# Four column pairs of an input projection as seven-product block multiplications, with two intermediate results kept in DRAM

## The chip, the core and the metric

The kernel runs as one program on 1 core of one Trainium2 chip. The metric is the device time of one execution in microseconds. TensorE (PE) multiplies matrices; its weight loads (PEld) overlap its matmuls. VectorE (DVE) and ScalarE (ACT) do the elementwise work, and SyncE (SP) issues the transfers. Each engine works through its own list of instructions in the order in which the program was compiled, and waits at an instruction until what it needs is there.

## The reference, cut to what matters

One encoder layer is applied to two groups of 256 tokens, which the kernel holds together as 512 tokens of width 1024. The changed part is the middle: one input projection of the normed activations `u`, whose columns feed a neighbourhood attention (q, k, v), a memory attention (q_m) and a state-space branch.

```python
x = x + 0.5 * swiglu(rms_norm(x, ffn1_norm), ffn1_w_gate, ffn1_w_up, ffn1_w_down)
u = rms_norm(x, mix_norm)
proj = u @ w_in
q_na, k_na, v_na, q_mem, z, xbc, dt_raw, gate_logits = split_sizes(proj, IN_SIZES)
...
o_na = neighborhood_attention(q_na, k_na, v_na, na_rpb)
...
o_mem = memory_attention(q_m, k_m, v_m)
g_na, g_ssd, g_mem = split_sizes(jax.nn.sigmoid(gate_logits), (D_MODEL, D_MODEL, D_MODEL))
merged = g_na * (o_na @ w_br_na) + g_ssd * (o_ssd @ w_br_ssd) + g_mem * (o_mem @ w_br_mem)
x = x + merged @ w_out
x = x + 0.5 * swiglu(rms_norm(x, ffn2_norm), ffn2_w_gate, ffn2_w_up, ffn2_w_down)
```

The q, k, v and q_mem columns are 4 x 1024 columns of `w_in`, 1024 rows deep.

## The kernel before

**Weights.** `PLAN` is a list of entries; each entry multiplies one or more weight chunks of 128 x 1024 numbers (`Item`). A chunk is loaded by SP into a ring of 9 buffers (`fetch`, `wr`), up to 8 items ahead. `ahead` splits it into a high part (`wh`, a cast on ACT, L332) and a low part (`wl`, a subtraction on DVE, L236), up to three items ahead of the one that is multiplied: the pool `pw` has 3 buffers of each. Every product is three matmuls: high by high, high by low, low by high.

**The two ways to multiply.** `quad` (L605 to L607) takes 512 columns: 4 chunks, 4 token blocks, 96 matmuls of 512 columns for 512 tokens by 1024 rows by 512 columns. The feed-forward layers use `product` (L583) instead: a pair of column blocks and a pair of token blocks are combined by seven products in place of eight. Sums of weight chunks are made in place on DVE (`sums`, `wr<-wr,wr`, L236), and the accumulating PSUM banks (`ac`) are shared by several products.

**The middle part.** After the memory's keys and values (`km`, `vm`, which read the memory tokens) and the 64 `dt` columns, eight `quad`s follow: qm 0, qm 1, v 0, v 1, q 0, k 0, q 1, k 1. Then come the memory gates and branches (`gate`, `br`), and after them the convolution columns.

**Background tasks.** Attention and norms are generators in a queue (`later`). `step` advances up to three active tasks by one part each. `run` calls it once after every plan entry, and `product` once more in its middle. The tasks here are `t_qkm` (norm and transposes of q_m, `tr`), `t_am` (memory attention of a head and a group: scores `am`, softmax `pm`, transposes `amT`, output `amo`), `t_qkn` (norms of q and k), `t_na` (neighbourhood attention of a pair of heads: transposes `qT` and `kT`, scaled query `qbd`, scores `ns`, softmax `nt`, transposes `nT`, copies `npT`, output `no`) and `t_dt` (the `dt` columns: `row`, `loc`). `require` runs tasks until those named are done.

**Order and buffers.** The Tile framework orders the instructions of each engine when the program is built. PSUM has 8 banks: 5 in pool `pm` (`m`, `q`, `ac`) and 3 in `pd` (all banks of tasks). Before, the outputs of the attention (`om`, `on`) are split where they are made, and stay in SBUF; so does the memory's v (`vm`). Four pairs of `on` borrow buffers of the weights' ring (`LEND`, `lent`).

Of the kernel before, what the change touches and what calls it, by code (L numbers as in the profile page):

```python
# [51 lines left out]
def seven(p, key, block, nh):  # L52
# [6 lines left out]
    for h in range(nh):  # L59
        n = lambda b: f"gu{key}.{h}.{b}"  # L60
# [6 lines left out]
        out.append(("gu", (*key, p, h, nh), [it]))  # L67
# [3 lines left out]
def make_plan():  # L71
# [10 lines left out]
    def ffn(f):  # L82
# [5 lines left out]
        for ci, (c0, w) in enumerate(CBLOCKS + ((DFF, 0),)):  # L88
# [7 lines left out]
            def part(p, ci=ci, c0=c0, w=w, n=n):  # L96
                s.extend(seven(p, (f, ci), lambda i, j, h: (f + ("_w_up", "_w_gate")[j], 4 * i + 4 // n * h, 4 // n, c0, w), n))
# [83 lines left out]
KEEP, EARLY, PG, LEND = 6, 4, 54, 4  # L181
TEMPS = set("rw e f e2 ca cb xt yq dg jk jn pm pmT nt npT bi st qbd kT nv mq ut mr a2h a2l s1 u2 p5 up sg af sf".split())


class Layer:
    def __init__(self, tc, ctx, aps):
# [20 lines left out]
        self.lent = 0  # L207
# [179 lines left out]
    def setup(self):  # L387
# [36 lines left out]
        self.scr_x = self.dr.tile([KD, 128, NT], F32, name="scr_x")  # L424
        self.scr_v = self.dr.tile([NT, D], F32, name="scr_v")
# [48 lines left out]
    def t_x(self, k):  # L474
# [24 lines left out]
        self.xs[7][k // 2] = self.split_tile(s7, "s")  # L499

# [66 lines left out]
    def product(self, p, h, nh, cis, w):  # L567
# [230 lines left out]
    def do_vm(self, key, cis):  # L798
# [4 lines left out]
        def evac():  # L803
            for t in range(4):
# [5 lines left out]
                self.o[("vm", key[0], t)] = r  # L810
# [48 lines left out]
    def t_am(self, h, b):  # L859
        qT, kT = self.o["qm"], self.o["km"]  # L860
# [29 lines left out]
        for ct in range(2):  # L890
            c0 = (h % 2) * 256 + ct * 128
            for kt in range(2):
                self.T.matmul(ps[:, ct * 256:(ct + 1) * 256], self.o[("vm", h // 2, 2 * b + kt)][:, c0:c0 + 128],  # L893
                              pT[:, kt * 256:(kt + 1) * 256], start=kt == 0, stop=kt == 1)
        for ct in range(2):
            k = ("om", 2 * h + ct)
            if k not in self.o:
                self.o[k] = (self.g(F32R, "omh"), self.g(F32R, "oml"))
            hi, lo = self.o[k]
            v = ps[:, ct * 256:(ct + 1) * 256]  # L900
            self.S.copy(hi[:, bs], v)
# [566 lines left out]
```

## Time and profile before

| | |
|---|---|
| median of 3 runs | 1736.32 us (1736.07 to 1737.01) |
| profiled execution, its own time | 1735.51 us |
| its span, first to last instruction | 1733.7 us |
| PE busy | 1724.5 us |
| DVE busy | 1225.5 us |
| ACT busy | 846.8 us |
| the eight quads, start to end | 456.8 to 682.2 us |
| memory gates and branches | 682.2 to 823.1 us |

The span is what the views divide up; the profiled execution's own time is 1.8 us longer, for what lies around the span. Busy matmuls overlap: each is listed with its whole duration, and the next starts before it ends.

### The profile page before, as it was taken

How to read it: one execution, taken by the hardware profiler on the slowest of the kernel's cores; microseconds unless marked ns; L12 is line 12 of the kernel's file. 1: busy time of each engine (PE TensorE's matmuls, PEld its weight loads, DVE VectorE, ACT ScalarE, POOL GpSimd, SP SyncE). 2: the span in 40 equal slices, each digit the busy share in tenths (PEclk: the TensorE clock that was granted, in tenths of full speed). 3: DMA queues.
4: the chain of work that ended last, by engine and by line, in shares of the span. 5: the costliest groups of instructions: out<-in, count | busy, mean ns of one | idle time of the engine just before them, and what ended most of it. 6: DMA issues, size and time to landing. Idle time of an engine off the chain costs nothing.

```text
span 1733.7 us, 22579 instructions
## 1 busy us (share of the span) xinstructions
PE 1724.5 (99%) x8556; PEld 1419.7 (82%) x8556; DVE 1225.5 (71%) x2057; ACT 846.8 (49%) x1515; POOL 0.8 (0%) x6
## 2 busy tenths in 40 slices
PE   9999999999999999999999999999999999999999
PEld 7888888988888887788878877877788878888887
DVE  7776776876255467845788898888853797776775
ACT  6543443543234336543656776767532564444442
POOL 0000000000000000000000000000000000000000
PEclk9999999999999999999999999999999999999999
DMA  7144234442323233333444544447443234244331
GB/s 273 59 136 146 97 110 134 158 156 82 99 87 96 87 109 91 99 104 98 122 127 128 145 131 120 152 128 200 158 134 121 73 124 132 86 146 133 98 109 49
DMA packets 79852, 209.75 MB, mean 121 GB/s; under 512 B 11136, under 2 KB 19840, under 8 KB 79744
## 3 DMA queue, kind: packets, MB, share of 16 engines
q1 hardware_dynamic: 79744, 208.32, 38.5%
q8 instruction: 67, 1.10, 0.3%
q14 instruction: 41, 0.34, 0.1%
HBM read 198.71 MB, written 9.58 MB: 120 GB/s over the span
## 4 chain that ended last, share of the span: by engine, by line
PE 97%; DVE 2%; ACT 0%; issue 0%; DMA 0%; POOL 0%; DVEq 0%; ACTq 0%; POOLq 0%
PE ac L583 21%; PE m L561 10%; PE m L563 10%; PE m L562 10%; PE q L605 5%; PE q L607 5%; PE q L606 5%; PE m L1110 5%; PE d L562 5%; PE d L563 5%; PE d L561 5%; PE y L1330 2%; PE hT L708 1%; PE am L865 1%; PE amo L893 1%; PE CB L1280 1%
## 5 line engine op out<-in xcount | busy, mean ns | idle before, releaser
L332 ACT CAST wh<-wr 128x1024 fp32r<-128x1024 f32 (+1 forms) x356 | 370.5, 1041 | 676.8 <-PE ac L583 166.5
L236 DVE TENSOR_TENSOR wl<-wr,wh 128x1024 fp32r<-128x1024 f32 (+1 forms) x356 | 430.6, 1210 | 256.6 <-ACT wh L332 243.9
L583 PE MATMUL ac<-wh,sh 128*128 128x512 f32 (+1 forms) x616 | 229.4, 373 | 0.5 <-ACT wh L332 0.5
L561 PE MATMUL m<-uh,wh 128*128 128x512 f32 x576 | 229.7, 399 | 0.0
L583 PE MATMUL ac<-wl,sh 128*128 128x512 f32 (+1 forms) x616 | 228.1, 370 | 0.7 <-DVE wl L236 0.7
L583 PE MATMUL ac<-wh,sl 128*128 128x512 f32 (+1 forms) x616 | 227.9, 370 | 0.0
L563 PE MATMUL m<-uh,wl 128*128 128x512 f32 x576 | 225.0, 391 | 0.0
L562 PE MATMUL m<-ul,wh 128*128 128x512 f32 x576 | 224.8, 390 | 0.0
L562 PE MATMUL d<-hl,wh 128*128 128x512 f32 x352 | 137.3, 390 | 0.7 <-DVE hl L236 0.7
L561 PE MATMUL d<-hh,wh 128*128 128x512 f32 x352 | 137.4, 390 | 0.5 <-ACT hh L258 0.5
L563 PE MATMUL d<-hh,wl 128*128 128x512 f32 x352 | 137.0, 389 | 0.0
L583 PEld LDWEIGHTS ac<-wl,sh 128*128 128x128 f32 x616 | 116.1, 189 | 20.7 <-DVE wl L236 1.3
L583 PEld LDWEIGHTS ac<-wh,sh 128*128 128x128 f32 x616 | 116.0, 188 | 20.5 <-ACT wh L332 1.3
L583 PEld LDWEIGHTS ac<-wh,sl 128*128 128x128 f32 x616 | 116.0, 188 | 19.6
L561 PEld LDWEIGHTS m<-uh,wh 128*128 128x128 f32 x576 | 108.2, 188 | 27.8 <-ACT ct L251 5.0
L563 PEld LDWEIGHTS m<-uh,wl 128*128 128x128 f32 x576 | 108.1, 188 | 23.5 <-issue 0.8
L562 PEld LDWEIGHTS m<-ul,wh 128*128 128x128 f32 x576 | 108.3, 188 | 21.8 <-issue 0.4
L247 DVE SCALAR_TENSOR_TENSOR x<-d,x 128x512 f32<-128x512 f32 x96 | 66.1, 689 | 76.6 <-PE d L563 76.1
L605 PE MATMUL q<-wh,uh 128*128 128x512 f32 x256 | 102.9, 402 | 0.0
L236 DVE TENSOR_TENSOR wr<-wr,wr 128x1024 f32<-128x1024 f32 x80 | 97.5, 1220 | 6.5 <-DMA wr<-in_w 5.4
L607 PE MATMUL q<-wl,uh 128*128 128x512 f32 x256 | 99.9, 390 | 0.0
L606 PE MATMUL q<-wh,ul 128*128 128x512 f32 x256 | 99.9, 390 | 0.0
(260 smaller groups left out, 2856.0 us busy)
## 6 DMA issues: line engine op xcount, KB each, us to landing
wr<-in_w SPq DMA_DIRECT2D x308, 512.0 KB
rw<-scr_r SPq DMA_DIRECT2D x64, 256.0 KB
nv<-scr_v SPq DMA_DIRECT2D x64, 64.0 KB
scr_o<-cv SPq DMA_DIRECT2D x12, 256.0 KB
or<-scr_o SPq DMA_DIRECT2D x12, 256.0 KB
wr<-in_w SPq DMA_DIRECT2D x9, 256.0 KB
x<-in_xT SPq DMA_DIRECT2D x8, 256.0 KB
mr<-in_memT SPq DMA_DIRECT2D x8, 256.0 KB
```

The source lines that it names most:

```text
L236: self.V.tensor_tensor(out=out, in0=a, in1=b, op=op)
L247: self.V.scalar_tensor_tensor(out=out, in0=a, scalar=s, in1=b, op0=op0, op1=op1)
L332: self.S.copy(hi[:, :n], t[:, :n])
L561: self.T.matmul(ps[:m], wh[:, kk, :], xh, start=i == 0, stop=False)
L562: self.T.matmul(ps[:m], wh[:, kk, :], xl, start=False, stop=False)
L563: self.T.matmul(ps[:m], wl[:, kk, :], xh, start=False, stop=i == n - 1)
L583: go = lambda l, r, **f: self.T.matmul(ps, l, r, skip_group_check=True, **f)
L605: self.T.matmul(self.qb[t], xh, wh[:, kk, :], start=k == 0, stop=False)
L606: self.T.matmul(self.qb[t], xl, wh[:, kk, :], start=False, stop=False)
L607: self.T.matmul(self.qb[t], xh, wl[:, kk, :], start=False, stop=k == KD - 1)
L1110: go = lambda l, r, **f: self.T.matmul(ps, l, r, skip_group_check=True, **f)
L1330: T.matmul(yb[64 * hp:64 * hp + 64, b * 256:(b + 1) * 256], xt[i][:, (2 * b + st) * 128 + 64 * hp:(2 * b + st) * 128 + 64 * hp + 64], w[hp ...
```

## The change

The eight quads become four sets of seven products, each for a pair of column blocks: (qm 0, qm 1), (v 0, v 1), (q 0, k 0), (q 1, k 1). A set is 14 plan entries (`sv`, seven products in two halves of the depth), and the seventh product of each set is issued after the first of the next; that of the last set stands after the first memory gate. Memory branches start two gates later. The token sums that products 5, 6, 3 and 7 need are made in `t_u` (`s_part`), before the `dt` columns. The memory's v goes to DRAM (`scr_m`), and `t_am` loads what it needs (`vl`). The outputs of both attentions are written to DRAM unsplit (`scr_b`), and `t_back` loads them and splits them later. The lending of ring buffers is gone. One product entry calls `step` twice, as in the feed-forward layers.

```diff
     quad("vm", 1, "w_mem_kv", 1536)
     a("dt", 0, "w_in", COL_DT, m=64)
-    quad("qm", 0, "w_in", COL_QM)
-    quad("qm", 1, "w_in", COL_QM + 512)
-    quad("v", 0, "w_in", COL_V)
-    quad("v", 1, "w_in", COL_V + 512)
-    for hf in range(2):
-        quad("q", hf, "w_in", 512 * hf)
-        quad("k", hf, "w_in", 1024 + 512 * hf)
+    sets = [("qm", 0, COL_QM, COL_QM + 512), ("v", 0, COL_V, COL_V + 512), ("qk", 0, 0, 1024), ("qk", 1, 512, 1536)]
+
+    def sv(i, p):
+        kind, c, *cols = sets[i]
+        s.extend(seven("sv", p, (kind, c), lambda i, j, h: ("w_in", 4 * i + 2 * h, 2, cols[j], 512), 2))
+
+    for i in range(4):
+        for p in PRODUCTS[:-1]:
+            sv(i, p)
+            if p == 1 and i:
+                sv(i - 1, 4)
     for j in range(8):
         gate("mem", j)
-        branch("mem", j)
+        if j == 0:
+            sv(3, 4)
+        if j > 1:
+            branch("mem", j - 2)
+    branch("mem", 6)
+    branch("mem", 7)
     light = [(f, j) for j in range(8) for f in (gate, branch)]
     for g in range(8):
         for i, (ct, col) in enumerate(((16 + g, COL_B + 128 * g), (24 + g, COL_C + 128 * g), (2 * g, COL_X + 256 * g),
...
         self.stt(lo, s2, -1.0, hi.bitcast(F32), ALU.mult, ALU.subtract)
         self.xs[3][k // 2] = (hi, lo)
         self.xs[7][k // 2] = self.split_tile(s7, "s")
+
+    def s_part(self, k, a, b):
+
+        half = lambda z: z[:, k % 2 * 256:k % 2 * 256 + 256]
+        if k % 2 == 0:
+            self.sf = [self.g(p="sf") for _ in range(4)]
+        s5, s2, s7, s3 = self.sf
+        self.tt(half(s5), b[:, 256:], a[:, 256:], ALU.subtract)
+        self.stt(half(s2), half(s5), -1.0, a[:, :256], ALU.mult, ALU.subtract)
+        self.tt(half(s7), a[:, :256], a[:, 256:], ALU.subtract)
+        self.stt(half(s3), half(s2), -1.0, b[:, :256], ALU.mult, ALU.subtract)
+        if k % 2:
+            for p, z in ((5, s5), (6, s2), (3, s3), (7, s7)):
+                self.su.setdefault(p, [None, None])[k // 2] = self.split_tile(z, "s")
+
+    def factor_of(self, p, k, t):
+
+        if self.base is None or p in self.su:
+            pair, c = (self.xs if self.base is None else self.su)[p][k // 2], k % 2 * 256
+        else:
+            k0, r = {1: (0, 0), 2: (4, 0), 4: (4, 1)}[p]
+            pair, c = self.base[k0 + k], 256 * r
+        return (z[:, c + t * 128:c + t * 128 + 128] for z in pair)
 
     def t_squares(self):
         for k in range(KD):
...
         yield from self.t_R(acc)
         yield
-        self.u = []
-        for k in range(KD):
-            t = self.g(p="ut")
-            self.stt(t, self.x[k], self.par("mix", k), self.R, ALU.mult, ALU.mult)
-            self.u.append(self.split_tile(t, "u"))
-            self.nc.sync.dma_start(out=self.scr_x[k], in_=self.x[k])
-            if k % 2:
-                yield
+        self.u = [None] * KD
+        for kk in range(4):
+            ts = {}
+            for k in (kk, kk + 4):
+                t = ts[k] = self.g(p="ut")
+                self.stt(t, self.x[k], self.par("mix", k), self.R, ALU.mult, ALU.mult)
+                self.u[k] = self.split_tile(t, "u")
+                self.nc.sync.dma_start(out=self.scr_x[k], in_=self.x[k])
+                self.x[k] = None
+            yield
+            self.s_part(kk, ts[kk], ts[kk + 4])
+            yield
         self.x = None
...
-                self.o[("vm", key[0], t)] = r
+                q = key[0]
+                self.nc.sync.dma_start(out=self.scr_m[t * 128:(t + 1) * 128, q * 512:(q + 1) * 512], in_=r)
...
 
-    def do_qm(self, key, cis):
-        qb = self.quad(key, cis, self.u)
-        if qb is None:
+    def pre_sv(self, key):
+        kind, c, p, h, nh = key
+        self.base = self.u
+        if p == 1 and h == 0:
+            self.gus[kind, c] = ({}, {})
+            self.o[kind, c] = [[None] * 4, [None] * 4]
+        if p == 4 and h == 0:
+            self.evacuate()
+        self.acc_ps = self.gus[kind, c][0]
+
+    def do_sv(self, key, cis):
+
+        kind, c, p, h, nh = key
+        o = self.gus[kind, c][1]
+        ps = self.product(p, h, nh, cis, 512)
+        if ps is None:
             return None
-        q = key[0]
+        if (kind, c) == ("qk", 1) and p in self.su:
+            self.su[p] = None
 
         def evac():
-            raw = []
-            for t in range(4):
-                r = self.g(p="qr")
-                (self.S.copy if t % 2 else self.V.tensor_copy)(r, qb[t])
-                raw.append(r)
-            self.later(("qm", q), self.t_qkm(raw, "mqn", self.o.setdefault("qm", {}), q))
-            for h in (2 * q, 2 * q + 1):
-                for b in range(2):
-                    self.later(("am", h, b), self.t_am(h, b), (("qm", q), ("km", q)))
-        evac()
+            for t in range(2):
+                v = ps[t]
+                if p in (1, 6, 5):
+                    y = o[p, t] = self.g(p={1: "s1", 6: "u2", 5: "p5"}[p])
+                    self.act(y, v, AF.Copy, scale=1.0 if p == 1 else -1.0)
+                    continue
+                r, j = {2: (0, 0), 7: (1, 1), 3: (0, 1), 4: (1, 0)}[p]
+                y = self.g(p="vr" if kind == "v" else "qr")
+                if p == 4:
+                    self.S.copy(y, v)
+                else:
+                    self.stt(y, v, 1.0 if p == 2 else -1.0, o.pop(({2: 1, 7: 5, 3: 6}[p], t)), ALU.mult, ALU.add)
+                if kind == "v":
+                    t0 = (2 * r + t) * 128
+                    self.nc.sync.dma_start(out=self.scr_v[t0:t0 + 128, j * 512:(j + 1) * 512], in_=y)
+                else:
+                    self.o[kind, c][j][2 * r + t] = y
+            if p in (7, 4) and kind != "v":
+                j = int(p == 7)
+                raw = self.o[kind, c][j]
+                if kind == "qm":
+                    self.later(("qm", j), self.t_qkm(raw, "mqn", self.o.setdefault("qmT", {}), j))
+                    for h in (2 * j, 2 * j + 1):
+                        for b in range(2):
+                            self.later(("am", h, b), self.t_am(h, b), (("qm", j), ("km", j)))
+                else:
+                    n = "qk"[j], c
+                    self.o[n] = raw
+                    self.later(n, self.t_qkn(raw))
+                    if p == 4:
+                        for pr in range(4 * c, 4 * c + 4):
+                            self.later(("na", pr), self.t_na(pr), (("q", c), ("k", c)))
+        return evac
 
     def t_qkm(self, raw, gain, dst, q):
         ss = self.small(8, "ss")
...
-        qT, kT = self.o["qm"], self.o["km"]
+        qT, kT = self.o["qmT"], self.o["km"]
+        vl = self.g(p="vl").rearrange("p (n c) -> p n c", n=2)
+        src = self.scr_m[b * 256:b * 256 + 256, h * 256:h * 256 + 256]
+        self.nc.sync.dma_start(out=vl, in_=src.rearrange("(n p) c -> p n c", n=2))
         bs = slice(b * 256, (b + 1) * 256)
         ps = self.bank("am")
         for qt in range(2):
...
+            k = 2 * h + ct
+            first = ("omr", k) not in self.o
+            if first:
+                self.o["omr", k] = self.g(p="omr")
+            r = self.o["omr", k]
+            self.S.copy(r[:, bs], ps[:, ct * 256:(ct + 1) * 256])
+            if not first:
+                self.nc.sync.dma_start(out=self.scr_b["om"][k], in_=self.o.pop(("omr", k)))
+
+    def t_back(self, n, ks):
+
+        raw = []
+        for k in ks:
+            raw.append(self.g(p="or"))
+            self.nc.sync.dma_start(out=raw[-1], in_=self.scr_b[n][k])
+        yield
+        yield
+        for k, r in zip(ks, raw):
+            self.o[n, k] = self.split_tile(r, "om")
...
-        if pr < LEND:
-            self.lent += 1
-            on = self.pf.tile([128, 1024], F32R, tag="raw", name=self.name("on"))
-            hi, lo = on[:, :512], on[:, 512:]
-        else:
-            hi, lo = self.g(F32R, "onh"), self.g(F32R, "onl")
-        self.o[("on", pr)] = (hi, lo)
 
...
             ov = ps[:, b * 256:(b + 1) * 256].rearrange("p (n r c) -> p n r c", n=4, r=4)
-            dst = lambda z: z[:, b * 256:(b + 1) * 256].rearrange("p (r n c) -> p n r c", r=4, n=4)
-            S.copy(dst(hi), ov)
-            self.tt(dst(lo), ov, dst(hi).bitcast(F32), ALU.subtract)
+            S.copy(on[:, b * 256:(b + 1) * 256].rearrange("p (r n c) -> p n r c", r=4, n=4), ov)
+        self.nc.sync.dma_start(out=self.scr_b["on"][pr], in_=on)
 
 
     def do_gate(self, key, cis):
...
+        if key == ("mem", 1):
+            tasks = [(("om", h), self.t_back("om", (2 * h, 2 * h + 1)), (("am", h, 0), ("am", h, 1)), -1) for h in range(4)]
+            self.queue.extendleft(reversed(tasks))
...
-            self.require(*[("am", h, b) for h in range(4) for b in range(2)])
+            self.require(*[("om", h) for h in range(4)])
             self.xo = [self.o.pop(("om", k)) for k in range(8)]
         else:
-            self.require(*[("na", p) for p in range(8)])
+            self.require(*[("on", p) for p in (0, 2, 4, 6)])
             self.xo = [self.o.pop(("on", k)) for k in range(8)]
 
     def do_br(self, key, cis):
...
+                if j == 7:
+                    self.xo = None
+                    for k in (0, 2, 4, 6):
+                        self.later(("on", k), self.t_back("on", (k, k + 1)), (("na", k), ("na", k + 1)))
                 return
             self.stt(t, t, 1.0, ps, ALU.add, ALU.mult)
             m = self.merged[j]
```

**The order on DVE in the neighbourhood attention.** DVE's list for the first three pairs before: `nt_...<-ns` is the first operation on a pair's scores, `nt<-nt,nm` the last one of its softmax, `wl` the low part of a weight chunk.

```order
L247 SCALAR_TENSOR_TENSOR nt_5348<-ns_5330,bi_5222 128x512
...
L1007 TENSOR_REDUCE nm_5353<-nt_5348 128x4
...
L1014 RECIPROCAL nm_5427<-nm_5350 128x4
...
L241 TENSOR_SCALAR nt_5349<-nt_5349,nm_5433 128x128 x4
...
L236 TENSOR_TENSOR wl_5486<-wr_4975,wh_5485 128x1024
L247 SCALAR_TENSOR_TENSOR nt_5458<-ns_5440,bi_5281 128x512
...
L241 TENSOR_SCALAR nt_5459<-nt_5459,nm_5533 128x128 x4
L236 TENSOR_TENSOR wl_5577<-wr_5040,wh_5576 128x1024
L247 SCALAR_TENSOR_TENSOR nt_5558<-ns_5540,bi_5385 128x512
...
L241 TENSOR_SCALAR nt_5559<-nt_5559,nm_5645 128x128 x4
L236 TENSOR_TENSOR wl_5674<-wr_5079,wh_5673 128x1024
```

And after the change, from the last weight chunk ahead of these pairs to the next one:

```order
L245 TENSOR_TENSOR wl_5865<-wr_5129,wh_5864 128x1024
...
L250 TENSOR_SCALAR qbd_5402<-qT_5397,params 128x256 x2
L256 SCALAR_TENSOR_TENSOR nt_5442<-ns_5424,bi_5360 128x512
...
L250 TENSOR_SCALAR qbd_5486<-qT_5481,params 128x256 x2
...
L256 SCALAR_TENSOR_TENSOR nt_5525<-ns_5507,bi_5395 128x512
...
L250 TENSOR_SCALAR nt_5526<-nt_5526,nm_5582 128x128 x4
...
L256 SCALAR_TENSOR_TENSOR nt_5606<-ns_5588,bi_5479 128x512
...
L250 TENSOR_SCALAR nt_5607<-nt_5607,nm_5671 128x128 x4
...
L256 SCALAR_TENSOR_TENSOR nt_5800<-ns_5782,bi_5687 128x512
...
L1056 TENSOR_REDUCE nm_5812<-nt_5801 128x4
L245 TENSOR_TENSOR wl_5910<-wr_5170,wh_5909 128x1024
```

Before, one weight chunk is split between one pair's softmax and the next one's; now three whole pairs and the first half of a fourth lie between two chunks.

**The order on PE at the same place.** Before, from the first pair's scores to the third's (`q` rows are the projection's matmuls; behind each of the two `kT` shown stand 24 of them, of which one is shown):

```order
L997 MATMUL ns_5330<-kT_5267,qbd_5229 64x128
...
L975 MATMUL kT_5366<-consts,kr_5109 128x128
...
L605 MATMUL q_5395<-wh_5234,uh_3211 128x512
...
L997 MATMUL ns_5440<-kT_5371,qbd_5288 64x128
...
L975 MATMUL kT_5476<-consts,kr_5109 128x128
...
L605 MATMUL q_5395<-wh_5293,uh_3259 128x512
...
L1023 MATMUL nT_5513<-consts,nt_5348 128x128 x4
L1023 MATMUL nT_5520<-consts,nt_5349 128x128 x4
L997 MATMUL ns_5540<-kT_5481,qbd_5392 64x128 x5
L997 MATMUL ns_5541<-kT_5481,qbd_5392 64x128 x5
```

After, from the first pair's scores to the third pair's transposes (`ac` are the projection's matmuls):

```order
L1046 MATMUL ns_5424<-kT_5381,qbd_5367 64x128 x2
...
L1031 MATMUL kT_5460<-consts,qr_5141 128x128
...
L1046 MATMUL ns_5507<-kT_5465,qbd_5402 64x128
...
L1031 MATMUL kT_5543<-consts,qr_5141 128x128
...
L1072 MATMUL nT_5562<-consts,nt_5442 128x128 x4
L1072 MATMUL nT_5569<-consts,nt_5443 128x128 x4
L1046 MATMUL ns_5588<-kT_5548,qbd_5486 64x128
...
L1082 MATMUL no_5630<-npT_5567,nv_5350 64x64
...
L1072 MATMUL nT_5651<-consts,nt_5525 128x128 x4
...
L1082 MATMUL no_5711<-npT_5656,nv_5385 64x64
...
L1072 MATMUL nT_5732<-consts,nt_5606 128x128 x4
L617 MATMUL ac_5405<-wh_5697,sh_3393 128x512
```

Before, 24 projection matmuls stand between one pair's scores and the next one's; now none stands from the first pair's scores to the first of the third pair's transposes, with three pairs' scores and two pairs' outputs between.

## Rows read from the trace of the kernel before

**Rows 1.** Page: busy time of the engines, and the chain that ended last.
```profile
PE 1724.5 (99%) x8556; PEld 1419.7 (82%) x8556; DVE 1225.5 (71%) x2057; ACT 846.8 (49%) x1515; POOL 0.8 (0%) x6
PE 97%; DVE 2%; ACT 0%; issue 0%; DMA 0%; POOL 0%; DVEq 0%; ACTq 0%; POOLq 0%
```

**Rows 2.** Timeline of PE in the quads; start, duration. 74 matmuls, first and last.
```profile
478.58 0.39 PE L606 MATMUL q<-wh,ul 128*128 128x512 f32 x1
...
495.13 0.39 PE L607 MATMUL q<-wl,uh 128*128 128x512 f32 x1
```

**Rows 3.** Windows: stretch, length; busy PE, PEld, DVE, ACT, POOL; clock; DMA share, GB/s.
```profile
456.80:682.20 225.40, 224.70 (x1161) 186.17 (x1159) 123.57 (x269) 86.81 (x203) 0.00 (x0) 1.00 0.30 94
682.20:823.10 140.90, 140.02 (x973) 114.39 (x973) 87.51 (x185) 64.55 (x157) 0.00 (x0) 1.00 0.34 102
823.10:1184.00 360.90, 360.90 (x1733) 291.07 (x1733) 305.20 (x619) 244.30 (x501) 0.00 (x0) 1.00 0.47 131
```

**Rows 4.** Groups by line, whole span, DVE: weight splits and sums; busy, mean ns.
```profile
L236 DVE TENSOR_TENSOR wl<-wr,wh 128x1024 fp32r<-128x1024 f32 x348 | 425.2, 1222 | 256.4 <-ACT wh L332 243.7 <-PE CB L1280 12.0
L236 DVE TENSOR_TENSOR wr<-wr,wr 128x1024 f32<-128x1024 f32 x80 | 97.5, 1220 | 6.5 <-DMA wr<-in_w 5.4
```

**Rows 5.** Timeline, neighbourhood attention of one pair: query, scores, transposes.
```profile
646.66 0.87 DVE L241 TENSOR_SCALAR qbd<-qT,params 128x256 f32<-128x256 f32 x2
650.05 1.10 PE L997 MATMUL ns<-kT,qbd 64*64 64x128 f32 x32
651.08 0.66 PE L975 MATMUL kT<-consts,kr 128*128 128x128 f32 x4
```

**Rows 6.** Timeline, one pair's softmax and what follows; start, duration.
```profile
660.77 1.28 DVE L247 SCALAR_TENSOR_TENSOR nt<-ns,bi 128x512 f32<-128x512 f32 x2
661.97 1.27 DVE L1007 TENSOR_REDUCE nm<-nt 128x4 f32<-128x512 f32 x2
662.67 0.40 ACT L251 ACTIVATE nt<-nt,nm 128x128 f32<-128x128 f32 x1 [1.76 <-DVE nm L1007]
...
664.23 0.39 ACT L251 ACTIVATE nt<-nt,nm 128x128 f32<-128x128 f32 x1
664.35 0.18 DVE L1014 RECIPROCAL nm<-nm 128x4 f32<-128x4 f32 x1 [1.12 <-ACT nt L251]
664.57 0.88 DVE L241 TENSOR_SCALAR nt<-nt,nm 128x128 f32<-128x128 f32 x4
665.50 1.03 PE L1023 MATMUL nT<-consts,nt 128*128 128x128 f32 x8
...
674.02 1.15 PE L1033 MATMUL no<-npT,nv 128*64 128x64 f32 x32
```

**Rows 7.** Timeline, one memory attention from scores to transposes.
```profile
511.85 1.89 PE L865 MATMUL am<-qkT,qkT 128*128 128x256 f32 x8
514.04 0.68 DVE L869 TENSOR_REDUCE mx<-am 128x2 f32<-128x512 f32 x1
...
516.28 0.61 DVE L241 TENSOR_SCALAR pm<-pm,mx 128x256 f32<-128x256 f32 x2
...
526.22 0.60 PE L884 MATMUL amT<-consts,pm 128*128 128x128 f32 x4
```

**Rows 8.** Groups on DVE, 456 to 682 us: the `dt` task.
```profile
L247 DVE SCALAR_TENSOR_TENSOR dt<-dt,dt 128x256 f32<-128x256 f32 x7 | 3.0, 424 | 0.0
L1183 DVE RECIPROCAL dt<-dt 128x256 f32<-128x256 f32 x1 | 1.7, 1747 | 0.0
```

**Rows 9.** Waits of PE on DVE in this part: us, times, longest.
```profile
PE qT L967 <- DVE nt L247: 0.7, 1, 0.7
PE kT L975 <- DVE kr L236: 0.7, 1, 0.7
```

**Rows 10.** Timeline of SP's queue: loads of v for one pair.
```profile
659.69 5.53 SPq L961 DMA_DIRECT2D nv<-scr_v  x8
```

**Rows 11.** Windows at the start, columns as in Rows 3.
```profile
1.00:3.00 2.00, 1.69 (x4) 1.42 (x5) 0.00 (x0) 1.21 (x2) 0.29 (x2) 1.00 0.41 77
```

More of the change, by code (lines that the diff above doesn't have):

```diff
@@ L49, in plain, with seven @@
     return add_item(n, nk, m, [(n, (mat, k0, nk, col, m))])
-def seven(p, key, block, nh):
+def seven(kind, p, key, block, nh):
     out = []
     for h in range(nh):
-        n = lambda b: f"gu{key}.{h}.{b}"
+        n = lambda b: f"{kind}{key}.{h}.{b}"
         blk = lambda b: block(int(b[1]) - 1, int(b[2]) - 1, h)
@@ L66, in seven @@
         it = add_item(n(src), nk, m, [(n(b), blk(b)) for b in loads], [tuple(n(b) for b in t) for t in sums])
-        out.append(("gu", (*key, p, h, nh), [it]))
+        out.append((kind, (*key, p, h, nh), [it]))
     return out
@@ L96, in part @@
             def part(p, ci=ci, c0=c0, w=w, n=n):
-                s.extend(seven(p, (f, ci), lambda i, j, h: (f + ("_w_up", "_w_gate")[j], 4 * i + 4 // n * h, 4 // n, c0, w), n))
+                s.extend(seven("gu", p, (f, ci), lambda i, j, h: (f + ("_w_up", "_w_gate")[j], 4 * i + 4 // n * h, 4 // n, c0, w), n))
             if f == "ffn1" and ci == 0:
@@ L178 @@
 NCONST = 128 * 9
-KEEP, EARLY, PG, LEND = 6, 4, 54, 4
-TEMPS = set("rw e f e2 ca cb xt yq dg jk jn pm pmT nt npT bi st qbd kT nv mq ut mr a2h a2l s1 u2 p5 up sg af sf".split())
+KEEP, EARLY, PG = 6, 4, 54
+TEMPS = set("vr vm vl omr onr or rw e f e2 ca cb xt yq dg jk jn pm pmT nt npT bi st qbd kT nv mq ut mr a2h a2l s1 u2 p5 up sg af sf".split())
 class Layer:
@@ L424, in setup @@
         self.scr_x = self.dr.tile([KD, 128, NT], F32, name="scr_x")
+        self.scr_m = self.dr.tile([NT, D], F32, name="scr_m")
+        self.scr_b = {n: self.dr.tile([8, 128, NT], F32, name="scr_" + n) for n in ("om", "on")}
         self.scr_v = self.dr.tile([NT, D], F32, name="scr_v")
@@ L581, in product @@
                 k = h * nk + kk
-                xh, xl = (z[:, k % 2 * 256 + t * 128:k % 2 * 256 + t * 128 + 128] for z in self.xs[p][k // 2])
+                xh, xl = self.factor_of(p, k, t)
                 go = lambda l, r, **f: self.T.matmul(ps, l, r, skip_group_check=True, **f)
@@ L890, in t_am @@
         for ct in range(2):
-            c0 = (h % 2) * 256 + ct * 128
             for kt in range(2):
-                self.T.matmul(ps[:, ct * 256:(ct + 1) * 256], self.o[("vm", h // 2, 2 * b + kt)][:, c0:c0 + 128],
+                self.T.matmul(ps[:, ct * 256:(ct + 1) * 256], vl[:, kt, ct * 128:ct * 128 + 128],
                               pT[:, kt * 256:(kt + 1) * 256], start=kt == 0, stop=kt == 1)
         for ct in range(2):
-            k = ("om", 2 * h + ct)
-            if k not in self.o:
-                self.o[k] = (self.g(F32R, "omh"), self.g(F32R, "oml"))
@@ L899, in t_am @@
-            hi, lo = self.o[k]
-            v = ps[:, ct * 256:(ct + 1) * 256]
-            self.S.copy(hi[:, bs], v)
-            self.sub_hi(lo[:, bs], v, hi[:, bs])
-    def do_v(self, key, cis):
-        qb = self.quad(key, cis, self.u)
-        if qb is None:
-            return None
-        q = key[0]
-        def evac():
-            for t in range(4):
-                r = self.g(p="vr")
-                (self.S.copy if t % 2 else self.V.tensor_copy)(r, qb[t])
-                self.nc.sync.dma_start(out=self.scr_v[t * 128:(t + 1) * 128, q * 512:(q + 1) * 512], in_=r)
-        evac()
@@ L918, in do_q @@
-    def do_q(self, key, cis, which="q"):
-        qb = self.quad(key, cis, self.u)
-        if qb is None:
-            return None
-        q = key[0]
-        def evac():
-            raw = []
-            for t in range(4):
-                r = self.g(p=which + "r")
-                (self.S.copy if t % 2 else self.V.tensor_copy)(r, qb[t])
-                raw.append(r)
-            self.o[(which, q)] = raw
-            self.later((which, q), self.t_qkn(raw))
-            if which == "k":
-                for pr in range(4 * q, 4 * q + 4):
-                    self.later(("na", pr), self.t_na(pr), (("q", q), ("k", q)))
-        evac()
@@ L937, in do_k @@
-    def do_k(self, key, cis):
-        return self.do_q(key, cis, "k")
+            k = 2 * h + ct
[15 more added lines that the diff above has]
+            self.o[n, k] = self.split_tile(r, "om")
```

9 lines of the change are left out of this document (5 added, 4 removed).

## The prediction

> **What bounds the kernel now.** I read the page first: PE is busy for 1724.5 of 1733.7 us, and 97% of the chain that ended last is PE [rows 1]. So a change pays only through PE's own work, and costs wherever it makes PE wait. The second view is PE's timeline in the quads. A matmul of 512 columns is listed with 0.39 us, but the starts show what one costs: from 478.58 to 495.13 us there are 73 intervals, so 16.55 / 73 = 0.2267 us each [rows 2]. The third is the windows by stage. The eight quads, the memory gates and the convolution columns keep PE busy for 224.70 of 225.40, 140.02 of 140.90 and 360.90 of 360.90 us, all at a granted clock of 1.00 (2.4 GHz) [rows 3]. DVE is busy for 123.57, 87.51 and 305.20 us there, so it has room in the first two; the third shows that PE need not wait even where DVE is 305.20 / 360.90 = 85% busy. The last is the waits of PE: the longest in this part are two of 0.7 us [rows 9]. There is hardly any stall to win back, so the change can win matmuls and can lose by new stalls.
>
> **What goes.** Eight quads hold 8 x 96 = 768 matmuls; four sets of seven products hold 4 x 7 x 24 = 672. The 96 that go are worth 96 x 0.2267 = 21.8 us. I add 1.0 for stalls of the quads that go with them (1.4 shown in rows 9). Together -22.8 us.
>
> **What comes on DVE, as a rate.** The sets split 56 chunks where the quads split 32, 24 x 1.222 = 29.3 us, and make 32 sums of chunks, 32 x 1.220 = 39.0 us [rows 4]. Eight evacuations more, which also add, are about 5 us at 0.64 each (two in 1.28) [rows 6]. The token sums come ahead of `dt`, where the memory products give DVE room, and I cost them at nothing; uncovered they would be some 12 us of DVE, at the nearest row's 0.42 for 256 columns [rows 8] and the splits. In the quads and memory gates DVE then works 123.57 + 87.51 + 73 = 284 us, in a stretch of 225.4 + 140.9 - 22 = 344 us: 83%, less than the 85% under which PE didn't wait [rows 3]. ACT's 24 more casts fit as well: it is busy for 151 of 366 us. By rate alone the gain would stand. What decides is the order, because each engine works through its list in order.
>
> **The neighbourhood attention in one clump.** An entry now calls `step` twice within 2.72 us (12 matmuls), where it called once in 5.44 us (24). The tasks thus lie about four times as densely. The two order lists show the result: DVE has three pairs and the first half of a fourth between two weight chunks, and PE has three pairs' scores and two pairs' outputs with no projection matmul between. So PE cannot fill the latency of a softmax any more. One pair's chain is: scores 1.10 [rows 5]; bias add 0.64 for the first half; reduction; exps from 662.67 to 664.62; reciprocal 0.18; scaling 0.88; transposes 1.03; copies; output 1.15 [rows 6]. From the bias add at 660.77 to the transposes at 665.50 it is 4.7 us for half a pair, with ACT's eight exps of 0.39 (3.1 us a pair) as the slowest link [rows 6].
>
> I laid these durations out by hand along both lists, from the end of the first pair's `qbd`. The second pair's `qbd` (0.87 [rows 5], ahead of the first bias add in DVE's list, and waiting for `qT`) ends at 3.3 us; the second pair is normalised at 11.6; the first output ends at 14.7, the second at 22.8; the fourth pair's scores at 27.4; 20 projection matmuls at 31.9; the last output at 36.9. PE's work in it is four scores (4.4), four outputs (4.6), four pairs of transposes (4.1), twenty `kT` and `qT` (3.3 at 0.66 for four) and 26 matmuls of 0.2267 (5.9), 22 us in all [rows 2, 5, 6]. PE waits for the other 15. With about 2 us ahead of it, for the norms of q and k which the first pair now follows at once, I take 17. The lower bound is 9: half a pair's 4.7 us twice, if two pairs overlap fully. The upper bound is 21: nothing of the softmax done ahead and 6 us for the norms. No weight chunk is split meanwhile, but three are ready ahead, so what is late next is only the tasks.
>
> **Smaller clumps.** The memory attention comes in two clumps with few matmuls between. After the scores a softmax takes from 513.74 to 516.89, 3.15 us; the transposes came at 526.22, so it was hidden [rows 7]. Uncovered twice it is 6.3 us; bounds 1 to 7, and I take 4, since a few matmuls remain. The `dt` task now runs in the first set: its reciprocal of 1.75 and seven operations of 0.42 are 4.7 us of DVE [rows 8], with `wl` queued behind them and PE waiting for that; bounds 2 to 7 (4.7 and two splits), taken 4. The first halves of products 5 want banks that product 2's evacuation frees: bounds 0 to 3 (four evacuations of 0.64), taken 1. The late branches and the outputs that come back from DRAM cost 0 to 5, taken 1: they were written long before, and eight loads of v for one pair pass SP's queue in 5.53 us [rows 10], which is the upper bound. Shifting the memory branches by two gates costs nothing: the same matmuls in other places.
>
> **Sum.** Stalls 17 + 4 + 4 + 1 + 1 = 27, less 22.8: +4.2 us. The profiled execution's own 1735.5 (span 1733.7 and 1.8 around it) becomes 1739.7. The median of the runs stands 0.8 above that execution, so I forecast 1740.5 us.
>
> **The rivals.** *A, the other side: the clumps are mostly absorbed.* If DVE and ACT run ahead of PE when the clump begins (their lists hold pair work that PE's last projection matmuls don't delay), each pair's softmax is partly done while PE still multiplies. All terms then take their low ends, 9 + 1 + 2 = 12 us, and the time is 1736.3 - 22.8 + 12 = 1725.5. For it: DVE's mean load of 83%. Against it: the `qbd` of the second pair stands ahead of the first bias add, and it needs PE's `qT` of the clump. It decides once all stalls together are under 19.3 us (22.8 less the 3.5 that is 0.2%).
>
> *B, PE's clock falls in the clump.* The granted clock is 1.00 in every stretch shown [rows 3], and even in the first us, where four records stand in 2 us [rows 11]; so no row shows a fall. At the lower level, 1.2 GHz, each matmul would cost another 0.2267 us by the ratio of the two levels; if the clump's 26 and the next 36 ran so, 62 x 0.2267 = 14 us, and the time would be 1754.5. The Trainium skill (TensorE: Matmul & The Clock Gate, Part 1: The HAM clock gate) says that the array is throttled to 1.2 GHz by default when idle and that activity releases it, which speaks against this change. PE is still 22 / 37 = 60% busy in the clump, though, and its single waits are a few us.
>
> *C, SP is late.* The returned outputs and the memory's v stand in SP's list behind loads that wait for buffers; two pairs' v ahead of a return are 2 x 5.53 = 11 us [rows 10], 1751.5 in all. Against it: they are issued many chunks before they are used.
>
> **How the numbers follow.** The forecast's case (stalls of about 17 to 36 us, 1731 to 1750) has 0.58, A 0.27, B 0.08, C 0.07. The range, 1725 to 1755, runs from A's value to B's; all terms at their upper ends (21 + 7 + 7 + 3 + 5 = 43) give 1756.5. Some 2 in 10 lies outside: an A with still less stall, and B or C on top of high ends. About 0.2% or 3.5 us is what a measurement can tell from no change, so faster is below 1732.8 and slower above 1739.8. Faster: A and 0.04 of the forecast's case, 0.31. Same: 0.22 of the forecast's case. Slower: 0.32 of it, B and C, 0.47.
>
> **What would show it.** In the changed kernel's profile: 672 `ac` at 0.2267 between starts in this part; PE idle some 15 us between the scores of the first pair and the output of the fourth, ended by DVE's `nt` and ACT's `npT`, and PE busy less than the span by about 27 us more than before; two short waits for `pm`, and one for `wl` behind `dt`. It is wrong if PE shows few gaps there (A), if the windows of the clump show a clock below 1.00 (B), or if PE's or DVE's longest waits are for `or` or `vl` (C).

## The result and the profile after

The changed kernel takes 1753.34 us (median of 4 runs, 1751.94 to 1755.36) where the kernel before takes 1736.34. The ratio is 1.0098, with an interval from 1.0081 to 1.0116: 17 us slower. The forecast was 1740.5, slower, with a range up to 1755.

The page of the changed kernel, lines that answer to [rows 1], and its granted clock in 40 slices:

```profile
PE 1718.6 (98%) x8460; PEld 1410.4 (81%) x8460; DVE 1301.8 (74%) x2129; ACT 893.0 (51%) x1579; POOL 0.8 (0%) x6
...
PEclk9999999999999987999999999999999999999999
...
PE 89%; DVE 5%; DMA 2%; ACT 1%; issue 1%; SPq 1%; DVEq 0%; ACTq 0%
```

Three things stand in these lines. PE has 96 instructions less (8556 to 8460), yet its busy time falls by only 5.9 us where 21.8 were removed. The granted clock is no longer full in two slices (8 and 7 tenths, from 613 to 701 us). And the chain leaves PE for 11% of the span, where it was 3%.

The windows of the changed kernel show where (columns as in [rows 3]):

```profile
457.00:500.00 43.00, 40.15 (x176) 31.30 (x175) 33.79 (x46) 19.47 (x29) 0.00 (x0) 0.96 0.35 107
500.00:620.00 120.00, 119.04 (x556) 98.05 (x556) 90.38 (x153) 64.02 (x131) 0.00 (x0) 1.00 0.44 144
620.00:690.00 70.00, 53.79 (x404) 43.23 (x402) 52.63 (x119) 35.46 (x98) 0.00 (x0) 0.78 0.38 120
690.00:860.00 170.00, 165.44 (x998) 135.10 (x998) 110.70 (x208) 85.74 (x187) 0.00 (x0) 1.00 0.45 147
```

PE is idle for 2.85, 0.96, 16.21 and 4.56 us, 24.6 in all; before it was 0.70, 0.88 and 0 in the stretches of [rows 3], 1.6. So there are 23.0 us of new idle time. In the first and third stretch the mean clock is 0.96 and 0.78: 40.15 x 0.04 and 53.79 x 0.22 are 1.6 and 11.8 us, so about 13 us are lost to work at the lower level. The span grew by 1752.0 - 1733.7 = 18.3; -21.8 + 23.0 + 13.4 is 14.6. I have no single place for the other 3.7: 1.4 of it lies ahead of the part (the first `ac` starts at 458.17 us, the first `q` did at about 456.8), and a matmul that follows a wait starts the next one later (0.60 us from 639.06 to 639.66 below, where the following ones take 0.43).

PE's timeline around the neighbourhood attention; start, duration, and in brackets the idle time before with what ended it:

```profile
633.35 0.39 PE L617 MATMUL ac<-wh,sl 128*128 128x512 f32 x1
633.58 0.61 PE L617 MATMUL ac<-wh,sh 128*128 128x512 f32 x2
639.06 0.80 PE L617 MATMUL ac<-wl,sh 128*128 128x512 f32 x1 [4.87 <-DVE wl L245]
639.66 0.63 PE L617 MATMUL ac<-wh,sl 128*128 128x512 f32 x1
640.08 0.63 PE L617 MATMUL ac<-wh,sh 128*128 128x512 f32 x1
640.51 0.63 PE L617 MATMUL ac<-wl,sh 128*128 128x512 f32 x1
...
643.48 0.39 PE L617 MATMUL ac<-wh,sh 128*128 128x512 f32 x1
643.71 0.39 PE L617 MATMUL ac<-wl,sh 128*128 128x512 f32 x1
...
651.95 1.20 PE L1046 MATMUL ns<-kT,qbd 64*64 64x128 f32 x32 [1.51 <-ACT kT L260]
654.96 1.09 PE L1031 MATMUL kT<-consts,qr 128*128 128x128 f32 x4 [1.80 <-DVE qbd L250]
655.84 1.06 PE L1023 MATMUL qT<-consts,qr 128*128 128x128 f32 x4
656.83 1.99 PE L1046 MATMUL ns<-kT,qbd 64*64 64x128 f32 x32
662.42 1.09 PE L1031 MATMUL kT<-consts,qr 128*128 128x128 f32 x4 [3.60 <-DVE qbd L250]
...
670.35 0.97 PE L1072 MATMUL nT<-consts,nt 128*128 128x128 f32 x4 [1.87 <-DVE nt L250]
...
675.61 1.97 PE L1082 MATMUL no<-npT,nv 128*64 128x64 f32 x30 [1.48 <-ACT npT L1074]
```

Before the wait of 4.87 us matmuls start 0.23 us apart; after it 0.43 (640.08 to 640.51), until they are back at 0.23 by 643.48. That is the clock at 1.2 and 2.4 GHz. A pair's scores take 1.99 us at the lower level against 1.10 in [rows 5]. From 654 to 681 us most of the work runs so.

In the first set the clock fell too, behind waits of 1.03, 1.14 and 0.68 us. The changed kernel there, and below it the run with eight gates first (described under the experiments), whose PE has the same list of instructions up to the memory attention and nearly the same waits (0.99, 1.14 and 0.65 us):

```profile
479.00:484.00 5.00, 4.99 (x14) 3.39 (x15) 2.19 (x4) 0.81 (x1) 0.00 (x0) 0.66 0.35 105
```

```profile
479.00:484.00 5.00, 5.00 (x24) 3.45 (x24) 3.55 (x7) 1.04 (x1) 0.00 (x0) 1.00 0.35 105
```

The loss comes in one execution and not in another: the memory attention begins at 515.6 us here and at 513.8 there. So 1.6 us or so between two profiles can be this alone.

What did the wait of 4.87 us stand for? DVE and SP in the same stretch, and DVE further on:

```profile
631.23 2.50 DVE L245 TENSOR_TENSOR qr<-qr,y 128x512 f32<-128x512 f32 x4
...
633.72 1.23 DVE L245 TENSOR_TENSOR wr<-wr,wr 128x1024 f32<-128x1024 f32 x1
634.85 0.20 DVE L285 TENSOR_TENSOR t<-y 128x32 f32<-128x32 f32 x1
636.91 0.43 DVE L245 TENSOR_TENSOR bi<-bi,consts 128x256 f32<-128x256 f32 x1 [1.86 <-DMA bi<-in_strip]
...
637.79 1.22 DVE L245 TENSOR_TENSOR wl<-wr,wh 128x1024 fp32r<-128x1024 f32 x1
...
658.24 0.43 DVE L245 TENSOR_TENSOR bi<-bi,consts 128x256 f32<-128x256 f32 x1 [1.64 <-DMA bi<-in_strip]
...
661.40 0.87 DVE L250 TENSOR_SCALAR qbd<-qT,params 128x256 f32<-128x256 f32 x2
...
667.39 0.76 DVE L245 TENSOR_TENSOR bi<-bi,consts 128x256 f32<-128x256 f32 x2 [2.75 <-DMA bi<-in_strip]
...
669.92 0.87 DVE L250 TENSOR_SCALAR nt<-nt,nm 128x128 f32<-128x128 f32 x4
```

```profile
625.84 6.55 SPq L1017 DMA_DIRECT2D nv<-scr_v  x8
632.43 0.66 SPq L1019 DMA_DIRECT2D bi<-in_strip  x1
```

The weight split `wl` that PE wants stands in DVE's list behind a norm (2.50 us), a sum of chunks (1.23) and the masked bias `bi`, and the bias is still on its way: SP issued it behind eight loads of v, at 632.43, and it served DVE at 636.91. So 1.86 of the 4.87 us is the bias, and the other 3.0 are work of the tasks and a sum that stand ahead of the split. The prediction gave the norms 2 us ahead of the clump; a late bias it had not priced. The same happens further on: the `qbd` for which PE waits 3.60 us and the `nt` for which it waits 1.87 come behind waits of DVE for the next biases, 1.64 and 2.75 us. The waits of DVE at the bias in the whole execution (us, times, longest), and those of PE at the returned outputs, from the views of waits:

```profile
DVE bi L245 <- DMA bi<-in_strip: 16.1, 7, 4.0
```

```profile
PE m L596 <- DVE oml L245: 2.1, 1, 2.1
...
PE m L595 <- ACT omh L267: 0.6, 1, 0.6
```

PE's wait of 2.1 us for the outputs' low parts `oml`, at the first memory branch, also stands behind a bias. No engine waits for the outputs' load from DRAM:

```profile
723.58 0.76 DVE L245 TENSOR_TENSOR bi<-bi,consts 128x256 f32<-128x256 f32 x2 [3.27 <-DMA bi<-in_strip]
...
726.17 3.70 DVE L245 TENSOR_TENSOR oml<-or,omh 128x512 fp32r<-128x512 f32 x6
```

### The profile page after: what moved, and what is told of

It is laid out like the page before. It is cut to its first block, busy times and chain, and to the rows that moved or that the text cites. A ratio compares the mean times of both kernels' runs of the same rounds, so it can differ in the third digit from the quotient of the medians.

```text
span 1752.0 us, 22664 instructions
## 1 busy us (share of the span) xinstructions
PE 1718.6 (98%) x8460; PEld 1410.4 (81%) x8460; DVE 1301.8 (74%) x2129; ACT 893.0 (51%) x1579; POOL 0.8 (0%) x6
## 4 chain that ended last, share of the span: by engine, by line
PE 89%; DVE 5%; DMA 2%; ACT 1%; issue 1%; SPq 1%; DVEq 0%; ACTq 0%
PE ac L617 25%; PE m L595 10%; PE m L597 10%; PE m L596 10%; PE m L1165 5%; PE d L596 5%; PE d L597 5%; PE d L595 5%; DVE wl L245 2%; PE y L1385 2%; PE q L639 2%; PE q L641 2%; PE q L640 2%; DMA wr<-in_w 1%; PE hT L743 1%
## 5 line engine op out<-in xcount | busy, mean ns | idle before, releaser
L341 ACT CAST wh<-wr 128x1024 fp32r<-128x1024 f32 (+1 forms) x380 | 396.8, 1044 | 656.8 <-PE ac L617 241.2
L245 DVE TENSOR_TENSOR wl<-wr,wh 128x1024 fp32r<-128x1024 f32 (+1 forms) x380 | 460.6, 1212 | 195.0 <-ACT wh L341 186.0
L617 PE MATMUL ac<-wl,sh 128*128 128x512 f32 (+1 forms) x744 | 280.8, 377 | 7.2 <-DVE wl L245 7.2
L617 PE MATMUL ac<-wh,sh 128*128 128x512 f32 (+1 forms) x744 | 281.3, 380 | 1.6 <-ACT wh L341 1.6
L617 PE MATMUL ac<-wh,sl 128*128 128x512 f32 (+1 forms) x744 | 279.8, 377 | 0.0
L617 PEld LDWEIGHTS ac<-wl,sh 128*128 128x128 f32 x744 | 141.3, 190 | 33.7 <-DVE wl L245 9.2
L617 PEld LDWEIGHTS ac<-wh,sl 128*128 128x128 f32 x744 | 141.2, 190 | 24.6
L245 DVE TENSOR_TENSOR wr<-wr,wr 128x1024 f32<-128x1024 f32 x112 | 136.8, 1222 | 9.0 <-DMA wr<-in_w 7.6
L260 ACT ACTIVATE e<-rw,lots 128x256 f32<-128x256 f32 (+1 forms) x256 | 97.6, 447 | 0.0
L256 DVE SCALAR_TENSOR_TENSOR cv<-m,params,cv 128x508 f32<-128x508 f32 (+1 forms) x128 | 95.4, 746 | 1.3
L596 PEld LDWEIGHTS d<-hl,wh 128*128 128x128 f32 x352 | 66.1, 188 | 14.8 <-DVE hl L245 1.4
```

Source lines behind the costliest of these rows:

```text
L245: self.V.tensor_tensor(out=out, in0=a, in1=b, op=op)
L256: self.V.scalar_tensor_tensor(out=out, in0=a, scalar=s, in1=b, op0=op0, op1=op1)
L260: self.S.activation(out=out, in_=x, func=f, **kw)
L341: self.S.copy(hi[:, :n], t[:, :n])
L596: self.T.matmul(ps[:m], wh[:, kk, :], xl, start=False, stop=False)
L617: go = lambda l, r, **f: self.T.matmul(ps, l, r, skip_group_check=True, **f)
```

## The experiments

All ratios are to runs of the kernel before on the same chip, whose median was between 1736.1 and 1736.5 us.

**First group.** *The bias ahead of v:*

```diff
+        bias = self.g(p="bi")
+        self.nc.sync.dma_start(out=bias, in_=self.a["strip"][pr])
         vt = [self.g(p="nv").rearrange("p (n c) -> p n c", n=4) for _ in range(2)]
...
-        bias = self.g(p="bi")
-        self.nc.sync.dma_start(out=bias, in_=self.a["strip"][pr])
```

> The bias of a pair is loaded ahead of its eight loads of v instead of behind them; nothing else differs from the changed kernel (1753.3 us). If the dense order itself makes PE wait (softmax chains without projection matmuls between), only DVE's own waits for the bias go, and the time falls by 2 to 5 us, to 1748 to 1751. If the late bias is the main cause (DVE stands at it with a weight split queued behind, and PE's clock falls in that wait), the longest wait of PE (4.87 us) goes with its clock loss and the later ones shorten: 1738 to 1745.

Measured: 1746.01 us (ratio 1.0058, 1.0043 to 1.0073), 7.3 less, between the two ranges. The wait for `wl` fell from 4.87 to 2.92 us and did not go; the wait for `oml` at the first memory branch went. So the late bias is one cause. How large a part it is this run doesn't tell, for two reasons. Half of the waits remain (DVE stands at the bias for 8.1 us in 4 waits, the longest 4.2, where it was 16.1 in 7). And in its profile the first set, ahead of any bias, ran at the full clock, which is some 1.6 us of the difference.

*One step for each entry of the sets:*

```diff
             if t == 0:
                 self.evacuate()
-                self.step()
-                self.n_slot += 1
+                if self.base is None:
+                    self.step()
+                    self.n_slot += 1
```

> The step in the middle of a product is left out in the four sets (kept in the feed-forward layers), so tasks are half as dense. If density is the cause, the waits in the neighbourhood attention and most of the clock loss go: some 20 us of the 24 us of idle and 16 us of slower matmuls come back, 1722 to 1736. If DVE's total work were the bound, the time would stay at 1748 to 1753. If late loads alone were the cause, about 1740, with the waits for the bias gone and the softmax chains still uncovered.

Measured: 1734.68 us (0.9991, 0.9981 to 1.0000), 18.7 less. DVE does the same work (1298.6 us busy against 1301.8), so its total work isn't the bound; of all single edits this one gives back most, so how densely the tasks lie is the largest cause. It thins out the loads as well: DVE's waits at the bias fall from 16.1 to 9.2 us. So this run doesn't separate the uncovered softmax chains from the loads that the dense tasks make late.

*q and k as quads* (the sets are cut to qm and v, the functions for quads are those of before), and *all columns as quads* (qm and v in the same way; the returns from DRAM stay, the token sums go):

```diff
-    for i in range(4):
+    for i in range(2):
         for p in PRODUCTS[:-1]:
             sv(i, p)
             if p == 1 and i:
                 sv(i - 1, 4)
+    sv(1, 4)
+    for hf in range(2):
+        quad("q", hf, "w_in", 512 * hf)
+        quad("k", hf, "w_in", 1024 + 512 * hf)
...
```

> Only qm and v are seven-product sets; q and k are quads as before; the returns from DRAM stay. The saving is 48 matmuls, 10.9 us. If the neighbourhood attention's density is the main loss, it is gone here, and what stays is the loss of the dt task in the first set (2.9 us of waits, some 2 of slower clock): 1736.3 - 10.9 + 5 = 1730, range 1727 to 1734. If the returns from DRAM or the memory attention cost much, 1738 or more.

> All eight column blocks are quads again; only the returns from DRAM, the memory branches two gates later and the missing lending of ring buffers stay. If these cost nothing: 1736.3 within 2 us. If the transfers by DRAM are late (rival C): 1740 to 1750.

Measured: 1740.71 (1.0027, 1.0018 to 1.0037) and 1744.31 (1.0047, 1.0032 to 1.0062). Both lie in the second of the two cases that were written down (1738 or more, and 1740 to 1750): all quads, with no seven-product set at all, are 8 us slower than before. So the rest of the change costs something that my prediction put at 1. That the transfers are late, as the second case says, is not what the waits show. PE's longest wait in the all-quad version and the one for the returned outputs, and DVE's at the bias:

```profile
PE kT L1082 <- DVE qbd L250: 4.9, 2, 4.1
...
PE m L596 <- DVE oml L245: 0.3, 1, 0.3
...
DVE bi L245 <- DMA bi<-in_strip: 14.9, 7, 3.6
```

The 4.1 us end at 733.9 us, at the first memory branches. There `require` asks for the returned outputs, and it steps all active tasks, neighbourhood pairs too, until they are there: a clump of its own, with late biases in it.

**Second group**, to tell the forced stepping from the bias. The edit "eight gates first" is

```diff
-        if j > 1:
-            branch("mem", j - 2)
-    branch("mem", 6)
-    branch("mem", 7)
+        if j > 7:
+            branch("mem", j - 8)
+    for j in range(0, 8):
+        branch("mem", j)
```

(`j` never passes 7 there, so all branches come from the second loop.)

*All quads, eight gates first; all quads, bias ahead of v:*

> All quads with the returns from DRAM (1744.3 us), and all eight memory gates ahead of the branches. If forced stepping ahead of the first memory branch is what made that version 8 us slower, 1735 to 1738; if the late bias loads alone did, it falls by no more than 3, to 1741 to 1744.

> All quads with the returns from DRAM, the gates as in that version, the bias loaded ahead of v. If late bias loads make the loss there (DVE stands at three of them for 2.1, 3.6 and 1.4 us), 1737 to 1739; if the forced stepping does, its softmax chains stay uncovered and it is 1741 to 1744.

Measured: 1736.02 (0.9999, 0.9990 to 1.0008) and 1740.81 (1.0025, 1.0014 to 1.0036). With eight gates' matmuls for the tasks to lie between, the whole of the 8 us is gone, and the returns from DRAM cost nothing. The edit also gives the transfers more time; that these were not the cost follows from the waits above (PE waited 0.3 us for the returned outputs). The bias alone gives back 3.5 us, so late biases are part of what the forced stepping costs. The windows of the all-quad version and of the one with eight gates first, in the same stretch (PE's busy time, clock, DMA share, GB/s):

```profile
700.00:740.00 40.00, 34.03 (x249) 0.96 0.51 167
```

```profile
700.00:740.00 40.00, 39.31 (x241) 1.00 0.55 180
```

PE's idle time there falls from 6.0 to 0.7 us, and the clock is full.

*One step and the bias ahead of v, without and with eight gates first:*

> One step for each entry of the sets, and the bias loaded ahead of v. With one step the version measured 1734.7 us and still shows PE waiting 2.5 us for a pair's transposes behind a late bias, 1.9 for a weight split behind the bias, and 2.7 for the normed q. If the bias is on the path of the first two, 1729 to 1732; if the softmax chain is, 1733 to 1736.

> As the run with one step and the bias first, and all eight memory gates ahead of the eight memory branches. If the forced stepping ahead of the first memory branch (tasks advanced with no matmuls between) costs time, 3 to 5 us less than that run, 1725 to 1729; if it costs nothing there, the same time.

Measured: 1730.72 (0.9971, 0.9961 to 0.9982) and 1729.34 (0.9962, 0.9948 to 0.9977). Both are faster than before. The 1.4 us between them is within their intervals: with one step little of the forced stepping was left. Without eight gates first, the bias ahead of v is worth 4.0 us at one step (1734.68 to 1730.72).

**Third group.** *The changed kernel with eight gates first, and nothing else:*

> The changed kernel (1753.3 us) with nothing else than all eight memory gates ahead of the eight branches. The prediction gave the branches and returns 1 us (0 to 5); the all-quad version got back 8.3 by this edit. If it is an effect of its own, 3.5 to 8 us come back, 1745 to 1750; if the dense steps ahead have eaten it already, 1752 to 1754.

Measured: 1749.03 (1.0075, 1.0060 to 1.0090), 4.3 less. The intervals just overlap, but the waits of 2.1 and 0.6 us at the first memory branch are gone from its profile. Some 1.6 us of the difference between the two profiles lies in the first set, which the edit doesn't touch (the two windows from 479 to 484 us above), so about 2.7 is left for the branches.

*The fastest version, with one more step between a pair's loads and its transposes:*

```diff
+        yield
         cs = slice(lp * 128, (lp + 1) * 128)
         ps = self.bank("qT")
```

> The fastest version so far (one step, bias first, eight gates first; 1729.3 us), and each pair waits one more step between its loads and its first transposes. If DVE's waits for the bias (2.6 and 2.8 us) and PE's wait for the normed q (2.7) are late inputs, most of the 8.7 us of waits between 637 and 655 us goes: 1721 to 1725. If the chain only moves, 1728 to 1731.

Measured: 1734.11 (0.9988, 0.9978 to 0.9997), 4.8 more: both cases missed, and the run shows something else. Windows of this version, and of the fastest before it, columns as in [rows 3]:

```profile
630.00:660.00 30.00, 21.86 (x135) 16.30 (x136) 21.12 (x46) 11.66 (x27) 0.00 (x0) 0.72 0.43 140
```

```profile
630.00:660.00 30.00, 21.62 (x170) 16.43 (x168) 24.48 (x54) 14.16 (x40) 0.00 (x0) 1.00 0.44 140
```

PE is idle for 8.1 and 8.4 us, the same. But in the first the waits left the clock at 0.72, and PE did 135 instructions where it does 170 at the full clock. 21.86 x 0.28 = 6.1 us of lower level, and the spans differ by 3.8 (1730.6 and 1726.8). With the idle time equal, the clock goes with the difference; the two also differ in the order of work, so this supports the price of the clock and doesn't isolate it.

*q and k as quads, eight gates first:*

> qm and v as sets, q and k as quads (1740.7 us), and all eight gates first. The all-quad version with this edit takes 1736.0; the two sets save 48 matmuls, 10.9 us, and lose what the first set showed, 2.9 us of waits and some 1.5 of slower clock, with about 1 at the transposes of q_m: 1730, range 1728 to 1732. If the sets save less than their matmuls elsewhere too, 1733 or more.

Measured: 1732.55 (0.9979, 0.9969 to 0.9989), 3.5 less than all quads with the same edit, where 48 matmuls are 10.9 us. Its waits in the first sets are 1.03, 1.13, 0.68 and 0.93 us, as in the changed kernel, with the clock at 1.00; with these 3.8 us the shortfall of 7.4 is half explained, and some 3.6 us aren't assigned.

*The fastest version, with the bias loaded one pair ahead:*

```diff
-        bias = self.g(p="bi")
-        self.nc.sync.dma_start(out=bias, in_=self.a["strip"][pr])
+        for n in (pr, pr + 1):
+            if ("bi", n) not in self.o and n // 4 == hf:
+                self.o["bi", n] = self.g(p="bi")
+                self.nc.sync.dma_start(out=self.o["bi", n], in_=self.a["strip"][n])
+        bias = self.o["bi", pr]
```

> The fastest version so far (one step, bias first, eight gates first; 1729.3 us), with each pair's bias loaded one pair ahead within a half, so that it no longer stands in SP's queue behind the v loads of the pair before. DVE's two waits for the bias (2.6 and 2.8 us) go. If they set PE's two waits for kT (2.0 and 2.3 us), 1724 to 1727; if the norms of q and k or the v loads hold the pairs anyway, 1728 to 1731.

Measured: 1727.94 us (0.9948, 0.9934 to 0.9962), 8.6 us faster than before, the best here. DVE's waits for the bias fall from 7.6 us in three to one of 2.4, and PE's longest wait stands right behind that one:

```profile
PE kT L1035 <- DVE nm L1067: 2.7, 1, 2.7
PE ac L617 <- DVE wl L245: 2.5, 2, 1.8
```

```profile
650.90 0.43 DVE L245 TENSOR_TENSOR bi<-bi,consts 128x256 f32<-128x256 f32 x1 [2.39 <-DMA bi<-in_strip]
651.25 0.87 DVE L250 TENSOR_SCALAR qbd<-qT,params 128x256 f32<-128x256 f32 x2
652.03 0.17 DVE L1067 RECIPROCAL nm<-nm 128x4 f32<-128x4 f32 x1
```

The reciprocal at 652.03 ends PE's wait of 2.7 us (PE goes on at 652.26); it stands in DVE's list behind the fourth pair's bias, which SP issued at 646.32, again behind eight loads of v. The gain of 1.4 lies within the intervals of the two, and a late bias still holds the pairs. What the softmax chains alone would cost isn't shown by any run here.

## Why the prediction came out as it did

**Direction and range were right, the likeliest case lacked 13 us.** The mechanism held in the main: the tasks lie too densely, PE waits for them, and this eats the matmuls saved. The idle time was nearly right as a sum, 27 less 1 forecast and 23.0 measured, but partly by luck: the memory attention was 3 us too large, the branches 2.4 too small, and in the largest term the causes differ from those that I priced. The range held because its top was rival B's value. The step that failed is the clock. The prediction costed every term at 1.00 and gave the fall a case of its own, rival B, at 1754.5 us and 0.08; it measured about 13 us against the 14 worked out there, and the time is 1753.3. I argued that PE stays 60% busy in the clump and that single waits are short. The rows show that this is no protection: the clock fell in the wait of 4.87 us, and again near 654 us, behind waits of 1.51 and 1.80. The Trainium skill (TensorE: Matmul & The Clock Gate, Part 1: The HAM clock gate) says in general that the default state is throttled and that activity releases it. The trace agrees, with a mean of 0.78 over 620 to 690 us, where PE was idle for 16.2.

**Term by term.**
- *Matmuls, -21.8:* right. 96 are gone, and those left start 0.23 us apart where nothing waits.
- *Neighbourhood attention, 17:* 16.2 us of idle between 620 and 690. The size is right, the cause only in part. The prediction put 15 on the softmax chains and 2 on the norms. 4.87 of it is a weight split behind a norm, a sum and a late bias, and two of the later waits, 3.60 and 1.87, come behind late biases as well. One step in place of two gave back 18.7 us, clock included, so density is the main part, as argued; how it divides between the chains and the late biases stays open. "What is late next is only the tasks" was wrong: a split and the biases were late too.
- *`dt`, 4:* 2.85 us of waits in the first set, inside the bounds. The 1.6 of clock on top came in this execution and not in that of the run with eight gates first.
- *Memory attention, 4:* at most 0.96 from 500 to 620 us, and that at the transposes of q_m (`tr`). Too large: PE never waits for `pm`.
- *Banks, 1:* no wait of PE in the profile names them.
- *Branches and returns, 1:* mis-sized. PE is idle for 3.4 us between 720 and 740, and eight gates first gave back 4.3 in the changed kernel (some 1.6 of it in the first set) and 8.3 with all quads. PE waits for no transfer of the outputs; the price is that `require` advances other tasks with no matmul between, and that their late biases hold up the splits of the outputs. I had read the placement and costed it at "the same matmuls in other places", without asking what is forced there.
- *Rate on DVE, no bound:* right; with the same work, one step and the bias first the kernel is faster than before (1730.72 us).

**Rivals.** A (absorbed) is wrong: 24.6 us of idle. B came true on top of the forecast's case. C named the right engine and the wrong transfer: SP is late with the bias (16.1 us of DVE's waits), not with the outputs or the memory's v. What stays open is a rest of some 2 us in the changed kernel and of 3.6 in the version with two sets, and the price of the softmax chains by themselves.

## What to carry to other kernels

When a change makes plan entries shorter, look at everything that is paced by entries: background tasks that advance once an entry lie closer together, and a `require` steps them with nothing between at all. Price a stall of TensorE twice, once as idle time and once as the work that runs at 1.2 GHz afterwards; as the second price comes in some executions and not in others (clock 0.66 and 1.00 behind the same waits here), give it a range. Small loads (here a bias behind eight loads of v) belong ahead of the big ones, since an in-order engine holds everything else behind them: this gave back 7.3, 4.0 and 3.5 us in three versions.

## What was not expected of the hardware

The granted clock fell although PE was busy for 53.79 of 70 us (620 to 690, clock 0.78). After the single wait of 4.87 us matmuls ran 0.43 us apart for some 4 us (639.06 to 643.48) before the spacing was 0.23 again. Two versions with 8.1 and 8.4 us of idle time in the same 30 us had clocks of 0.72 and 1.00, so the sum of the idle time does not tell whether the clock falls. Nor do the single waits: behind 1.03, 1.14 and 0.68 us the clock was 0.66 from 479 to 484 us, and behind 0.99, 1.14 and 0.65 us in the same instructions of another run it was 1.00. One `bi` load was served 4.5 us after SP issued it (632.43 to 636.91), and the eight loads ahead of it kept SP for 6.55 us.
